# Column sums by way of device memory instead of a TensorE fold, and a twelve-pass lead before each product in halves

## Chip, cores and metric

The program runs on one NeuronCore of a Trainium2 chip. The metric is device time in microseconds (us) of one execution. Three runs of the kernel before took 979.87, 979.88 and 977.43 us, median 979.87. Line numbers such as L113 are lines of the kernel's file; the names of tiles are those of the program.

## What is computed

A two-layer trunk on 256 tokens of width 1024, in fp32. Each layer has a half-step SwiGLU FFN (width 2816), a token mixer (a causal spatial gating part beside sparse attention over selected tokens), and a second FFN. Each of the three is normalised before, shifted and scaled before, and gated behind, by vectors that come from a conditioning vector c:

```python
c_act = jax.nn.silu(c)
for l in range(DEPTH):                                  # DEPTH = 2
    mod = c_act @ ada_w[l] + ada_b[l]                   # (1, 9 * 1024)
    sh1, sc1, g1, sh2, sc2, g2, sh3, sc3, g3 = jnp.split(mod, 9, axis=-1)
    h = modulate(rms_norm(x, norm_ffn1[l]), sh1, sc1)   # h * (1 + scale) + shift
    x = x + 0.5 * g1 * swiglu(h, ffn1_w_in[l], ffn1_w_out[l])
    h = modulate(rms_norm(x, norm_mix[l]), sh2, sc2)
    x = x + g2 * token_mix(h, cos, sin, mix_w_in[l], sgu_w[l], sgu_b[l], mix_w_out[l])
    h = modulate(rms_norm(x, norm_ffn2[l]), sh3, sc3)
    x = x + 0.5 * g3 * swiglu(h, ffn2_w_in[l], ffn2_w_out[l])
return rms_norm(x, final_norm)
```

## The kernel before

**Tiles and phases.** The 256 tokens are two row blocks b = 0, 1 of 128, which stay on the chip in x. Six phases follow each other: FFN 1, mixer and FFN 2 of layer 0, then of layer 1. A matrix product in fp32 is made as three passes of rounded operands (mm3, L594): with hi a rounded copy and lo the remainder, hi x hi, hi x wlo and lo x whi are added up in one PSUM bank. So each weight tile arrives by DMA (raw), is cast by ScalarE to whi (L535) and has its remainder wlo made by VectorE (L540). At most ten such pairs (NB) are in use, seven raw tiles (NRAW) in flight.

**FFN.** It has two stages. In the first, chunks of 512 or 256 columns of w_in are multiplied for gate and up parts. Most are "joint chunks": the weight tile stands still in the PE array, the transposed tokens of both row blocks (256 columns) move, and one matmul takes about 0.11 us. In all phases but the first, one chunk is done apart for each row block, with the weights moving in 512 columns (L741). Its results, transposed, are aThi and aTlo. The second stage ("a-stage") is the down-projection w_out: 22 k-blocks x 2 row blocks x 2 halves of 512 columns x 3 passes, the activations standing and the weights moving. It is written in project (L682), which takes one k-block after another, the second row block some blocks behind the first (LAG), and does the last three (TAIL) half by half so that the update of x can start on one half while the other is multiplied. In the very last down-projection the second row block has its 1024 columns cut in 512, 256 and 256 (PARTS, L601).

**Order of columns in a pass.** For projections the kernel uses mm3r (L577). Its moving operand and its PSUM target are read in an order of their own, by runs (L572): four runs, each of 16 groups of 8 columns, shown as 4x16x8. Twice a row is otherwise: a "product in halves" (L580 to L584) has its first pass in plain order, its second cut in two matmuls of 256 columns, its third by runs. The counter T.n tells whether any other matmul has come between. Behind such a break the first product is done by runs and the next in halves, and on an unbroken stream a product in halves comes every 48 passes (PERIOD). The mixer's projections, other than its output, use plain mm3.

**Modulation vectors.** Sixteen of the 18 vectors (each 1024 long) are made while the phases run; the first two at the start. Their weights are units in the same sequence as the layer weights (weave, L300): eight tiles of 128x1024 a vector, multiplied by c on VectorE into one accumulator aacc (L522; the first of the eight on ScalarE, L517). What is left then is a sum over the 128 partitions of aacc. The kernel before makes it in three steps: VectorE reduces groups of 32 with a transpose (fold_rows, L409; L414), giving a 128x32 tile; TensorE multiplies that with fold, a matrix that adds up the four groups (L430 for a gate, L462 for a shift or scale); VectorE takes the result out of PSUM. Shift and scale vectors go into ab, laid along partitions (L466 to L470). A gate vector gets its bias added, is written to device memory as one row and read back to all partitions by the POOL queue (L433 to L437), giving vec, which update (L644) multiplies with.

**What sets the order.** Each engine runs its instructions in the order in which the program issues them (the schedule is manual). The program is a loop of items: an item is one step of a row block or one step of a joint chunk. Work that must come later is deferred by a number of items (defer, L355), and FOLD_D = (2, 2, 10) are such numbers: the reduce two items behind the last accumulate, the fold ten items behind the reduce. Tiles hThipad and hTlopad are three small slots of 32 columns each, taken in turn. SyncE's queue carries the weights; ScalarE's and POOL's queues carry little.

## Time and profile before

| | us |
|---|---|
| median of three runs | 979.87 |
| the profiled execution, its own time | 978.13 |
| the profiled execution, span from first to last instruction | 976.4 |
| start and first FFN's chunks, 0 to 147.91: length, PE busy | 147.91, 139.73 |
| mixer of layer 0, 209.60 to 322.29: length, PE busy | 112.69, 112.58 |
| FFN 2 chunks of layer 0, 322.29 to 437.41: length, PE busy | 115.12, 115.12 |
| FFN 1 chunks of layer 1, 498.37 to 620.73: length, PE busy | 122.36, 122.36 |
| mixer of layer 1, 681.00 to 793.00: length, PE busy | 112.00, 111.89 |
| FFN 2 chunks of layer 1, 793.00 to 908.37: length, PE busy | 115.37, 115.37 |
| behind the last down-projection, 969.00 to 976.40: length, PE busy | 7.40, 0.38 |

The four down-projections lie between these rows. Over the span the DMA engines moved 253.47 MB, 260 GB/s on average. PE is TensorE's matmuls, PEld its weight loads, DVE is VectorE, ACT ScalarE, POOL GpSimd, SP SyncE. A row of the trace in order of time has the start in us, the duration in us, the engine, the line, the operation, the tiles (out<-in) and the shapes. The durations of neighbouring matmuls overlap, so what a matmul costs is read from one start to the next.

### The profile page before, as it was taken

The page shows a single profiled execution, that of the slowest core. Times are in us where ns is not written, and L with a number is a line of the kernel's source. Part 1 is how long each engine was busy: PE and PEld are TensorE (multiplying, and loading weights), DVE is VectorE, ACT ScalarE, POOL GpSimd, SP SyncE. Part 2 cuts the span into 40 slices and gives each one's busy share as a digit, 9 for nine tenths or more (in the row PEclk, how much of TensorE's full clock was granted, in tenths as well). Part 3 has the DMA queues.
Part 4 walks back from the last instruction along what each step waited for, and adds up shares of the span by engine and source line. Part 5 has one row for each costly group of instructions (what it writes and reads, how often), then busy time and mean ns, then how long its engine had stood idle before and what let it go on. Part 6 is the DMA issues. An engine that isn't in the chain of part 4 may idle for free.

```text
span 976.4 us, 16690 instructions
## 1 busy us (share of the span) xinstructions
PE 961.0 (98%) x6448; PEld 866.6 (89%) x6448; DVE 768.7 (79%) x1072; ACT 530.1 (54%) x794; POOL 54.8 (6%) x92
## 2 busy tenths in 40 slices
PE   7999999999999999999999999999999999999997
PEld 6899998887888899998889999988777889999886
DVE  6889899788998888786587898767899886656444
ACT  6565555375676754553366554345657775444331
POOL 4012400000000100000000100000000000000000
PEclk9999999999999999999999999999999999999999
DMA  9989999967665799897868999885765557777431
GB/s 330 393 277 364 337 385 377 413 178 230 185 181 172 229 329 348 314 328 252 262 185 299 329 332 318 302 301 173 246 189 184 170 175 250 247 239 235 151 129 43
DMA packets 110416, 253.47 MB, mean 260 GB/s; under 512 B 9138, under 2 KB 27620, under 8 KB 110336
## 3 DMA queue, kind: packets, MB, share of 16 engines
q1 hardware_dynamic: 108256, 248.06, 74.6%
q0 software_dynamic: 1792, 3.82, 1.2%
q8 instruction: 50, 0.82, 0.3%
q10 hardware_dynamic: 288, 0.52, 0.1%
q14 instruction: 30, 0.25, 0.1%
HBM read 251.30 MB, written 1.07 MB: 258 GB/s over the span
## 4 chain that ended last, share of the span: by engine, by line
PE 85%; DVE 6%; DMA 4%; issue 2%; ACT 1%; POOL 0%; SPq 0%; POOLq 0%; DVEq 0%; ACTq 0%
PE bank L113 83%; PE bank L117 2%; DMA raw<-in_ffn_w_in_dram 2%; DVE wlo L540 2%; DMA sraw<-in_ada_w_dram 1%; DVE aacc L1195 1%; DVE aacc L522 1%; ACT whi L535 1%; DMA raw<-in_ada_w_dram 1%; DVE xm L645 0%; DVE xm L635 0%; DVE x L647 0%; DVE wlo L481 0%; POOL rstd L618 0%; DVE hTlo L641 0%
## 5 line engine op out<-in xcount | busy, mean ns | idle before, releaser
L535 ACT ACTIVATE whi<-raw 128x1024 fp32r<-128x1024 f32 (+1 forms) x328 | 340.2, 1050 | 261.9 <-PE bank L113 167.1
L540 DVE TENSOR_TENSOR wlo<-raw,whi 128x1024 fp32r<-128x1024 f32 (+1 forms) x313 | 375.1, 1211 | 112.1 <-ACT whi L535 110.6
L113 PE MATMUL bank<-hThi,whi 128*128 128x256 f32 x1216 | 325.0, 278 | 1.4 <-ACT hThi L1233 0.9
L113 PE MATMUL bank<-hThi,wlo 128*128 128x256 f32 x1216 | 322.0, 276 | 0.0
L113 PE MATMUL bank<-hTlo,whi 128*128 128x256 f32 x1216 | 322.0, 276 | 0.0
L113 PEld LDWEIGHTS bank<-hThi,whi 128*128 128x128 f32 x1216 | 222.4, 188 | 3.5 <-ACT hThi L1233 1.5
L113 PEld LDWEIGHTS bank<-hTlo,whi 128*128 128x128 f32 x1216 | 222.1, 188 | 0.1
L113 PEld LDWEIGHTS bank<-hThi,wlo 128*128 128x128 f32 x1216 | 222.0, 188 | 0.0
L522 DVE SCALAR_TENSOR_TENSOR aacc<-raw,ccol,aacc 128x1024 f32<-128x1024 f32 x112 | 143.5, 1281 | 0.0
L113 PE MATMUL bank<-whi,aThi 128*128 128x512 f32 (+1 forms) x374 | 141.0, 377 | 0.0
L113 PE MATMUL bank<-whi,hThi 128*128 128x512 f32 (+1 forms) x352 | 140.4, 399 | 0.0
L113 PE MATMUL bank<-wlo,aThi 128*128 128x512 f32 (+1 forms) x404 | 140.1, 359 | 0.0
L113 PE MATMUL bank<-whi,aTlo 128*128 128x512 f32 (+1 forms) x374 | 139.8, 374 | 0.0
L113 PE MATMUL bank<-whi,hTlo 128*128 128x512 f32 (+1 forms) x352 | 135.4, 385 | 0.2
L113 PE MATMUL bank<-wlo,hThi 128*128 128x512 f32 (+2 forms) x374 | 134.3, 369 | 0.0
L113 PEld LDWEIGHTS bank<-wlo,aThi 128*128 128x128 f32 x404 | 75.9, 188 | 13.0
L113 PEld LDWEIGHTS bank<-wlo,hThi 128*128 128x128 f32 x374 | 70.5, 188 | 12.1
L113 PEld LDWEIGHTS bank<-whi,aTlo 128*128 128x128 f32 x374 | 70.3, 188 | 11.1
L113 PEld LDWEIGHTS bank<-whi,aThi 128*128 128x128 f32 x374 | 70.2, 188 | 10.9
L113 PEld LDWEIGHTS bank<-whi,hTlo 128*128 128x128 f32 x352 | 66.1, 188 | 14.0 <-DVE hTlo L641 1.1
L113 PEld LDWEIGHTS bank<-whi,hThi 128*128 128x128 f32 x352 | 66.3, 188 | 13.6 <-issue 2.0
L798 DVE TENSOR_TENSOR xm<-xm,bank 128x256 f32<-128x256 f32 x76 | 29.6, 417 | 38.8 <-ACT xm L797 38.8
(166 smaller groups left out, 680.9 us busy)
## 6 DMA issues: line engine op xcount, KB each, us to landing
raw<-in_ffn_w_in_dram SPq DMA_DIRECT2D x160, 512.0 KB, 5.4
raw<-in_ada_w_dram SPq DMA_DIRECT2D x128, 512.0 KB, 5.5
raw<-in_ffn_w_out_dram SPq DMA_DIRECT2D x88, 512.0 KB, 5.8
raw<-in_mix_w_in_dram SPq DMA_DIRECT2D x40, 512.0 KB, 4.4
sraw<-in_ada_w_dram SPq DMA_DIRECT2D x32, 256.0 KB, 5.8
raw<-in_ffn_w_in_dram SPq DMA_DIRECT2D x32, 256.0 KB, 4.2
raw<-in_mix_w_out_dram SPq DMA_DIRECT2D x16, 512.0 KB, 4.1
vec<-gline POOLq DMA_DIRECT2D x6, 512.0 KB, 7.2
```

Of the source, the lines that this page charges most:

```text
L113: return nc.tensor.matmul(*a, **kw)
L117: return nc.tensor.transpose(*a, **kw)
L522: V.scalar_tensor_tensor(aacc, e["raw"], ccol[:, j:j + 1], aacc, op0=ALU.mult, op1=ALU.add)
L535: S.activation(hi[:, :n], src, AF.Copy)
L540: V.tensor_tensor(lo[:, :n], src, hi[:, :n].bitcast(F32), op=ALU.subtract)
L798: V.tensor_tensor(a, a, acc[j][:, 256:], op=ALU.mult)
L1195: V.scalar_tensor_tensor(acc, su[g][j], ccol[:, j:j + 1], su["dps"] if j == PEJ else acc, op0=ALU.mult, op1=ALU.add)
```

## The change

**Column sums.** The matrix fold and its setup are gone. column_sums takes the place of fold_rows: VectorE's transposing reduce (now with columns in another order), then the 128x32 tile R is written to device memory (part), read back with another layout (L419) so that the four groups lie side by side in one partition, and VectorE adds them up (L425). Each of these steps is deferred: FOLD_D = (2, 2, 5, 6) stands for the items up to the reduce, the write, the read-back and the sum. Vectors for shift and scale use POOL's queue for the two transfers, gates ScalarE's. A gate then adds its bias (from cols, no longer loaded apart), is scattered to a row in device memory with elements of 4 bytes (gline, L438), and is read to all partitions two items later (vec, L443), on SyncE's queue in layer 1 and for the third gate of layer 0, on POOL's otherwise. The first two gates of layer 0 wait four items more before the sum (GL). In layer 1 the vectors of FFN 2 are woven to end 12 units earlier (FL).

**Order of columns.** In mm3r, a break now puts SETTLE = 4 products of plain order (twelve passes) ahead, then one product in halves, then runs up to the next break; PERIOD is gone. The mixer's output projection uses mm3, so plain order all through. In the last down-projection the second row block uses two halves of 512 like the others; its second half is cut at the last three k-blocks: what has been added up is put into x early (update), and the three last k-blocks go into fresh banks of 512, 256 and 256 columns.

```diff
-PERIOD = 48
+SETTLE = 4
-FOLD_D = (2, 2, 10)
+FOLD_D = (2, 2, 5, 6)
+GL = 4
+FL = 12
...
-        seq += weave(u3, vl[2], F0, F1)
+        seq += weave(u3, vl[2], F0, F1 - FL * l)
...
-    def fold_rows(acc, then):
-        R = spare_tile(0)
-        blocks = acc.rearrange("p (j r) -> p j r", r=32)
+    def column_sums(acc, eng, then, late=0):
+        R, C = spare_tile(0), spare_tile(1)
 
         def red():
-            V.tensor_reduce(R, blocks, axis=AX.X, op=ALU.add, apply_transpose=True)
-            then(R)
+            V.tensor_reduce(R.rearrange("p (m k) -> p m k", m=4),
+                            acc.rearrange("p (k r m) -> p m k r", m=4, r=32),
+                            axis=AX.X, op=ALU.add, apply_transpose=True)
+            defer(FOLD_D[1], there)
+
+        def there():
+            part = dramp.tile([P, 32], F32, name="part", tag="part")
+            eng.dma_start(part, R)
+            defer(FOLD_D[2], lambda: back(part))
+
+        def back(part):
+            eng.dma_start(C.rearrange("p (g k) -> p g k", g=4),
+                          part.rearrange("(g r) (m k) -> (r m) g k", g=4, m=4))
+            defer(FOLD_D[3] + late, total)
+
+        def total():
+            cs = small.tile([P, KD], F32, name="cs", tag="cs")
+            V.tensor_reduce(cs, C.rearrange("p (g k) -> p k g", g=4), axis=AX.X, op=ALU.add)
+            then(cs, C)
         defer(FOLD_D[0], red)
...
+        def put(cs, C):
+            V.tensor_tensor(C[:, :KD], cs, cols[:, l, v * KD:(v + 1) * KD], op=ALU.add)
+            defer(FOLD_D[1], lambda: out(C))
+
+        def out(C):
+            line = dramp.tile([1, D], F32, name="gline", tag="gline")
+            S.dma_start(line.rearrange("o (k p) -> p (o k)", p=P), C[:, :KD])
+            defer(FOLD_D[2], lambda: spread(line))
+
+        def spread(line):
+            t = vecp.tile([P, D], F32, name="vec", tag="vec")
+            (nc.sync if l or v == 8 else G).dma_start(t, line.to_broadcast([P, D]))
+            vec[(l, "G", v // 3 + 1)] = t
+        column_sums(acc, S, put, GL if l == 0 and v < 8 else 0)
...
-        fresh = T.n != stream[0]
-        if ps.shape[-1] == 512 and not first and (fresh or stream[1] >= PERIOD):
+        if T.n != stream[0]:
+            stream[1] = -SETTLE
+        if stream[1] < 0:
+            mm3(ps, ahi, alo, whi, wlo, first, last)
+        elif stream[1] == 0 and ps.shape[-1] == 512 and not first:
...
             T.matmul(runs(ps), alo, runs(whi), start=False, stop=last)
-            stream[1] = 0
         else:
             mm3(runs(ps), ahi, alo, runs(whi), runs(wlo), first, last)
-            if fresh:
-                stream[0], stream[1] = -1, PERIOD
-                return
-        stream[0] = T.n
-        stream[1] += 3
+        stream[:] = T.n, stream[1] + 1
...
-        parts = PARTS if final and b == 1 else HALF
+        parts, cut = HALF, final and b == 1
...
+            own = cut and h > 0
+            (mm3r if n == KF else mm3)(
+                acc[h], ahi, alo, w[0][:, 0, parts[h]], w[1][:, 0, parts[h]],
+                k == 0 or own and k == n - TAIL, k == n - 1 or own and k == n - TAIL - 1)
...
+        if cut:
+            update(b, l, i, acc[1], HALF[1])
+            give(bk.pop())
+            parts = PARTS
+            bk += [take(), take()]
+            acc = [t[:, :sl.stop - sl.start] for t, sl in zip(bk, parts)]
```

**What moves, in TensorE's order.** First the start of the first FFN's down-projection in layer 0, behind the last joint chunk (the rows `bank<-hThi,wlo`). Before, with L113 the line of the matmul:

```order
L113 MATMUL bank_86<-hThi,wlo 128x256
L113 MATMUL bank_83<-whi,aThi 128x4x16x8
L113 MATMUL bank_83<-wlo,aThi 128x4x16x8
L113 MATMUL bank_83<-whi,aTlo 128x4x16x8
L113 MATMUL bank_80<-whi,aThi 128x4x16x8
L113 MATMUL bank_80<-wlo,aThi 128x4x16x8
L113 MATMUL bank_80<-whi,aTlo 128x4x16x8
L113 MATMUL bank_83<-whi,aThi 128x512
L113 MATMUL bank_83<-wlo,aThi 128x256 x2
L113 MATMUL bank_83<-whi,aTlo 128x4x16x8
L113 MATMUL bank_80<-whi,aThi 128x4x16x8
```

Now, from the third product on (the two ahead of it have the same form in the same two banks; lines are now those of the changed file, where the matmul is L115):

```order
L115 MATMUL bank_86<-whi,aThi 128x512
L115 MATMUL bank_86<-wlo,aThi 128x512
L115 MATMUL bank_86<-whi,aTlo 128x512
L115 MATMUL bank_82<-whi,aThi 128x512
L115 MATMUL bank_82<-wlo,aThi 128x512
L115 MATMUL bank_82<-whi,aTlo 128x512
L115 MATMUL bank_86<-whi,aThi 128x512
L115 MATMUL bank_86<-wlo,aThi 128x256 x2
L115 MATMUL bank_86<-whi,aTlo 128x4x16x8
L115 MATMUL bank_82<-whi,aThi 128x4x16x8
```

Before, the second product behind the joint chunk is the one in halves; now four plain products (two in each bank) stand ahead of it. Second, the same down-projection some ten products later in TensorE's order, where the first gate's fold stood. Before:

```order
L113 MATMUL bank_80<-whi,aThi 128x4x16x8
L113 MATMUL bank_80<-wlo,aThi 128x4x16x8
L113 MATMUL bank_80<-whi,aTlo 128x4x16x8
L113 MATMUL bank_82<-fold,hThipad 32x32
L113 MATMUL bank_83<-whi,aThi 128x512
L113 MATMUL bank_83<-wlo,aThi 128x256 x2
L113 MATMUL bank_83<-whi,aTlo 128x4x16x8
L113 MATMUL bank_80<-whi,aThi 128x4x16x8
L113 MATMUL bank_80<-wlo,aThi 128x4x16x8
L113 MATMUL bank_80<-whi,aTlo 128x4x16x8
```

Now, at about the same place, from the product in halves that follows the transposition of cols (L1254, which breaks the stream in both kernels):

```order
L115 MATMUL bank_86<-whi,aThi 128x512
L115 MATMUL bank_86<-wlo,aThi 128x256 x2
L115 MATMUL bank_86<-whi,aTlo 128x4x16x8
L115 MATMUL bank_82<-whi,aThi 128x4x16x8
L115 MATMUL bank_82<-wlo,aThi 128x4x16x8
L115 MATMUL bank_82<-whi,aTlo 128x4x16x8
L115 MATMUL bank_80<-whi,aThi 128x4x16x8
L115 MATMUL bank_80<-wlo,aThi 128x4x16x8
L115 MATMUL bank_80<-whi,aTlo 128x4x16x8
```

The row with fold is gone, and with it the product in halves behind it; the stream goes on by runs. Third, the gate's way. Before, POOL's order for the first two gates of layer 0 (in_ada_b_dram is the bias, hTlopad the small tile that becomes the row):

```order
L420 DMA hTlopad<-in_ada_b_dram 32x32 x2
L435 DMA gline<-hTlopad 32x32
L437 DMA vec<-gline 128x1024
L435 DMA gline<-hTlopad 32x32
L437 DMA vec<-gline 128x1024
L618 TENSOR_TENSOR rstd<-ms,mhalf 128x1 x4
```

Now the row starts on ScalarE's queue, between the weight casts and the FFN's activations (part and gline lie in device memory):

```order
L557 ACTIVATE aThi<-xm_107 128x512
L523 ACTIVATE whi<-raw 128x1024
L1252 ACTIVATE cols<-bank_83 128x96
L415 DMA part<-hThipad 128x32
L523 ACTIVATE whi<-raw 128x1024
L505 ACTIVATE aacc<-raw,ccol 128x1024
L523 ACTIVATE whi<-raw 128x1024
L419 DMA hTlopad<-part 128x4x8
L523 ACTIVATE whi<-raw 128x1024
L438 DMA gline<-hTlopad 128x8x1
L523 ACTIVATE whi<-raw 128x1024 x5
L438 DMA gline<-hTlopad 128x8x1
```

What were four transfers of POOL's queue for the two gates behind the bias loads are now three transfers of ScalarE's for each gate, ahead of casts that the weights wait for; the two broadcasts (vec) stay on POOL's queue.

More of the change, by code (lines that the diff above doesn't have):

```diff
@@ L151, in trunk @@
     V.memset(negm, 1.0)
-    fold = const.tile([P, P], F32, name="fold")
     mconst = const.tile([P, 16], F32, name="mhalf")
-    mhalf, quarter = mconst[:, :1], mconst[:, 4:8]
+    mhalf = mconst[:, :1]
     G.memset(mhalf, -0.5)
-    def fold_setup():
-        V.tensor_reduce(quarter, ident.rearrange("p (a c) -> p a c", a=4), axis=AX.X, op=ALU.add)
-        V.tensor_reduce(fold[:, :32], ident.rearrange("p (a c) -> p c a", a=4), axis=AX.X, op=ALU.add)
-        V.tensor_copy(fold[:, 32:].rearrange("p (a c) -> p a c", a=3),
-                      fold[:, None, :32].to_broadcast([P, 3, 32]))
     def causal_mask():
@@ L416, in fold_rows @@
         defer(FOLD_D[0], red)
-    def bias_row(e):
-        row = spare_tile(1)[:32]
-        G.dma_start(row, ada_b[e["l"], e["v"] * D:(e["v"] + 1) * D].rearrange("(j r) -> j r", r=32))
-        accs.append(row)
     def ada_finish(e, acc):
         l, v = e["l"], e["v"]
-        row = accs.pop()
-        def go(R):
-            def prod():
-                ps = tp_tile()
-                T.matmul(ps[:32, :32], R, fold[:, :32], start=True, stop=True)
-                def put():
-                    V.tensor_tensor(row, ps[:32, :32], row, op=ALU.add)
-                    line = dramp.tile([1, D], F32, name="gline", tag="gline")
-                    G.dma_start(line.rearrange("o (j r) -> (o j) r", r=32), row)
-                    t = vecp.tile([P, D], F32, name="vec", tag="vec")
-                    G.dma_start(t, line.to_broadcast([P, D]))
-                    vec[(l, "G", v // 3 + 1)] = t
-                evac_later(EV_D, put)
-            defer(FOLD_D[2], prod)
-        fold_rows(acc, go)
+        def put(cs, C):
+            V.tensor_tensor(C[:, :KD], cs, cols[:, l, v * KD:(v + 1) * KD], op=ALU.add)
+            defer(FOLD_D[1], lambda: out(C))
@@ L458, in col_finish @@
     def col_finish(e, acc, late):
-        def go(R):
-            def prod():
-                ps = tp_tile()
-                T.matmul(ps[:, :32], fold, R, start=True, stop=True)
-                def put():
-                    Rk = R.rearrange("p (k m) -> p k m", m=4)
-                    V.tensor_tensor(Rk, ps[:, :32].rearrange("p (k m) -> p k m", m=4),
-                                    quarter[:, None, :].to_broadcast([P, KD, 4]), op=ALU.mult)
-                    cs = small.tile([P, KD], F32, name="cs", tag="cs")
-                    V.tensor_reduce(cs, Rk, axis=AX.X, op=ALU.add)
-                    col_bias(e["l"], e["v"] // 3 + 1, e["kind"], cs, 0)
-                evac_later(EV_D, put)
-            defer(FOLD_D[2] + late, prod)
-        fold_rows(acc, go)
+        column_sums(acc, G, lambda cs, C: col_bias(e["l"], e["v"] // 3 + 1, e["kind"], cs, 0), late)
     late = []
@@ L1339, in start @@
         causal_mask()
-        fold_setup()
     gens = {}
```

3 lines of the change are left out of this document (removed).

## The prediction, before the result was known

> **What bounds the kernel now.** I read the page first: the share of each engine, then the chain that ended last.
>
> ```profile
> span 976.4 us, 16690 instructions
> PE 961.0 (98%) x6448; PEld 866.6 (89%) x6448; DVE 768.7 (79%) x1072; ACT 530.1 (54%) x794; POOL 54.8 (6%) x92
> PE 85%; DVE 6%; DMA 4%; issue 2%; ACT 1%; POOL 0%; SPq 0%; POOLq 0%; DVEq 0%; ACTq 0%
> ```
>
> TensorE is covered for 961.0 of 976.4 us and carries 85% of the chain. It rarely waits, so the time is the sum of the distances from one matmul's start to the next, and an edit counts through the matmuls that it removes and the pace of those that stay. The second view is the busy time by stage, cut at the four FFN down-projections ("a-stages": 264 passes each of 512 columns, 22 k-blocks x 2 row blocks x 2 halves x 3 passes). Behind the stretch stand its length, the busy time (and count) of PE, PEld, DVE, ACT and POOL, the granted clock, the DMA share and GB/s.
>
> ```profile
> 147.91:209.60 61.69, 61.69 (x288) 51.08 (x287) 53.30 (x60) 32.25 (x42) 2.70 (x5) 1.00 0.92 348
> 437.41:498.37 60.96, 60.96 (x286) 50.85 (x284) 41.43 (x48) 27.22 (x36) 2.70 (x5) 1.00 0.78 254
> 620.73:681.00 60.27, 60.27 (x285) 50.97 (x284) 41.76 (x50) 26.80 (x36) 1.62 (x3) 1.00 0.76 247
> 908.37:969.00 60.63, 60.63 (x340) 52.71 (x339) 28.81 (x33) 18.83 (x25) 1.94 (x3) 1.00 0.32 105
> ```
>
> PE never rests there and the granted clock is 1.00, yet the pace is not one number. The third view, TensorE in order of time, shows why. A row "128x256 f32 x2" is a product in halves. From one such row to the next, unbroken, lie 48 passes' worth of work.
>
> ```profile
> 153.34 0.24 PE L117 MATMUL bank<-ident,vec 96*128 96x96 f32 x1
> 153.68 0.40 PE L113 MATMUL bank<-wlo,aThi 128*128 128x256 f32 x2
> 154.93 0.25 PE L113 MATMUL bank<-fold,hThipad 128*32 128x32 f32 x2
> 155.44 0.40 PE L113 MATMUL bank<-wlo,aThi 128*128 128x256 f32 x2
> 166.04 0.40 PE L113 MATMUL bank<-wlo,aThi 128*128 128x256 f32 x2
> 168.61 0.25 PE L113 MATMUL bank<-fold,hThipad 128*32 128x32 f32 x2
> 169.12 0.40 PE L113 MATMUL bank<-wlo,aThi 128*128 128x256 f32 x2
> 180.34 0.40 PE L113 MATMUL bank<-wlo,aThi 128*128 128x256 f32 x2
> 191.39 0.40 PE L113 MATMUL bank<-wlo,aThi 128*128 128x256 f32 x2
> ...
> 204.57 1.04 PE L117 MATMUL bank<-ident,xm 128*128 128x128 f32 x8
> 205.68 0.41 PE L113 MATMUL bank<-wlo,aThi 128*128 128x256 f32 x2
> ```
>
> 155.44 to 166.04 is 10.60 us, 220.8 ns a pass (its halved product included). 169.12 to 180.34 is 11.22 us, 233.8 ns. 180.34 to 191.39 is 11.05 us, 230.2 ns. The same instructions on the same shapes run at three paces, and the pace changes only at a product in halves. So that product chooses a pace, and the stream keeps it until the next one.
>
> What does the choice hang on? Compare a stream that had been running evenly with one just broken. The joint chunks run evenly up to the a-stages at 437.41, 620.73 and 908.37. The product in halves behind each, and one behind a fold:
>
> ```profile
> 439.04 0.40 PE L113 MATMUL bank<-wlo,aThi 128*128 128x256 f32 x2
> 448.20 0.25 PE L113 MATMUL bank<-fold,hThipad 128*32 128x32 f32 x2
> ...
> 479.61 0.40 PE L113 MATMUL bank<-wlo,aThi 128*128 128x256 f32 x2
> 490.82 0.40 PE L113 MATMUL bank<-wlo,aThi 128*128 128x256 f32 x2
> ...
> 622.36 0.40 PE L113 MATMUL bank<-wlo,aThi 128*128 128x256 f32 x2
> 631.52 0.25 PE L113 MATMUL bank<-fold,hThipad 128*32 128x32 f32 x2
> ...
> 910.00 0.40 PE L113 MATMUL bank<-wlo,aThi 128*128 128x256 f32 x2
> 918.40 0.28 PE L113 MATMUL bank<-whi,aThi 128*128 128x256 f32 x1
> ```
>
> Behind the joint chunks 41 passes take 9.16 us, twice the same to 10 ns, and 38 take 8.40 us: 221 to 223 ns, the fast pace all three times (the slow one would need 9.59 us for 41). One pass behind a break anything comes: fast at 155.44, slow at 169.12 and at 479.61 (11.21 us to 490.82).
>
> **The change part by part.** First the lead: behind every break twelve contiguous passes run before the product in halves. Whether contiguous passes settle is seen in the mixer, which runs them already:
>
> ```profile
> 260.26 0.48 PE L113 MATMUL bank<-whi,hThi 128*128 128x512 f32 x1
> ...
> 261.49 0.39 PE L113 MATMUL bank<-whi,hTlo 128*128 128x512 f32 x1
> ...
> 264.21 0.39 PE L113 MATMUL bank<-whi,hTlo 128*128 128x512 f32 x1
> ```
>
> 261.49 to 264.21 is 12 passes in 2.72 us, 226.7 ns without change. So twelve of them bring the stream to one known state, and every product in halves behind them should choose the same pace. No row shows that pace: ends 220.8 and 233.8 ns. I take 220.8, since the settled streams nearest to it, the three above, all went there. 264 passes at 220.8 are 58.29 us a stage. The lead costs 12 x (226.7 - 220.8) = 0.07 us a site, two sites in the middle stages, three in the first, one in the last. Where the eight transposes break a stream, 204.57 to 205.68 is 1.11 us for them and one pass, 0.89 more than a pass, in three stages. The column transpose of the first (153.34 to 153.68) costs 0.12. Stage by stage: 59.51, 59.32, 59.32 and 58.36, the last with 0.1 for its 18 half-width passes at the end: 58.46. Sum 236.6. Before, the four stretches sum to 243.55, and the last ran on some 0.2 us: 243.8. **-7.2 us.** That holds the seven folds inside the stages and the last stage's 256-column passes, which become 512 wide.
>
> Second, the folds go from TensorE. Seven lie in the a-stages and are counted. Six break joint chunks, three the mixer.
>
> ```profile
> 393.44 0.30 PE L113 MATMUL bank<-hThipad,fold 128*128 128x32 f32 x2
> 393.58 0.36 PE L113 MATMUL bank<-hThi,whi 128*128 128x256 f32 x1
> 393.78 0.28 PE L113 MATMUL bank<-hTlo,whi 128*128 128x256 f32 x1
> 393.89 0.28 PE L113 MATMUL bank<-hThi,wlo 128*128 128x256 f32 x1
> ```
>
> 393.44 to 393.78 is 0.34 us for two fold passes and one of the chunk's own, which takes 0.11 in an even stretch (393.78 to 393.89): 0.23 us each. Nine of them: **-2.1 us.**
>
> Third, the mixer's output projection becomes contiguous throughout, and the first FFN chunk gets short leads. One of their longest streams now:
>
> ```profile
> 311.59 0.40 PE L113 MATMUL bank<-wlo,hThi 128*128 128x256 f32 x2
> 322.29 1.03 PE L117 MATMUL bank<-ident,xm 128*128 128x128 f32 x8
> ```
>
> 10.70 us for 47 passes is 227.7 ns: where contiguous passes stand as well. I take 0. If all of some 480 such passes moved to an end of the three paces, it would be -3 or +3 us.
>
> Fourth, VectorE, and the queues.
>
> ```profile
> L414 DVE TRANSPOSE_TENSOR_REDUCE hThipad<-aacc 128x32 f32<-128x1024 f32 x16 | 19.8, 1238 | 0.0
> L469 DVE TENSOR_REDUCE cs<-hThipad 128x8 f32<-128x32 f32 x10 | 1.9, 186 | 0.3
> L466 DVE TENSOR_TENSOR hThipad<-bank,mhalf 128x32 f32<-128x32 f32 x10 | 1.9, 185 | 0.0
> gline<-hTlopad POOLq DMA_DIRECT2D x6, 4.0 KB, 3.6
> 150.00:160.00 10.00, 10.00 (x49) 8.23 (x48) 10.00 (x13) 6.84 (x12) 0.00 (x0) 1.00 1.03 413
> ```
>
> A shift or scale vector loses the 185 ns product and keeps a reduce of the 186 ns kind; a gate vector gains one. That is hidden under TensorE's 98%. The transposing reduce reads another order: 1.24 us as now, at most twice that by my estimate, 16 times. Each vector adds a write and a strided read-back, a gate a scattered write in place of the 3.6 us one. The reads are collected 6 items later (a pass group of 1.3 us in an a-stage, 2.7 us in a chunk), so 8 to 16 us stand against landings of a few us, and the first layer's gates get 4 items more. Behind a waiting ACT issue queue the weight casts, behind POOL's the rstd powers, behind VectorE's sum the weight remainders. I take 0; the far end is in the third rival.
>
> Sum: 978.13 (the profiled execution's own time) - 7.2 - 2.1 = **968.8, called 969**. The runs shown have a median of 979.87, 1.7 above that execution, so a median behind the change may lie as much higher.
>
> One rule speaks against the first term. The Trainium skill (TensorE: Matmul & The Clock Gate, section Back-to-back issue gap) gives a warm pass as columns / 2.4 + 2.5 ns, so 216 ns for 512 whatever stood before it. The rows above differ, 220.8 and 233.8 ns, so here the measurement decides. By that rule no pace could be chosen, and the time would be that of rival 4.
>
> **The rivals.** (1) The settled lead meets the wrong pace, the same one eight times over, since the site is the same. For: no row shows a contiguous lead before halves, and 169.12 shows that the slow pace stays until the next product in halves, of which the change leaves only one per break. 935 passes behind the leads x 13.0 ns = 12.2 us on the forecast: **981.0**, slower than before; at the middle pace 977.6. It decides from 968.8 to 978.13, so at 9.3 us / 935 = 10 ns a pass, above 230.8 ns. Against: three settled starts of three were fast.
>
> (2) One long stream is lost. A 208-pass stream in the first layer follows the column transpose, and a single wait of TensorE can shift it with no later product to mend it. 208 x 9 to 13 ns is 2 to 3 us, with a second stream of 232 some 5: **973**.
>
> (3) The first layer starves. At 150 to 160 us VectorE stands at 10.00 of 10 and the DMA share at 1.03, so no room hides more. Five vectors end there. If a gate's round trip costs the weights as much as a 3.6 us landing and a column vector half of that, and twice 1.2 us of slower reduce is added, it is 2 x 3.6 + 3 x 1.8 + 2.4 = 15 us of delay against the chunk's prefetch; I estimate that 6 of it shows: **975**, 984 if all did. The Trainium skill (DMA: Bandwidth & Descriptors, section Specifications) counts transfers under 512 B as read-modify-write; the gate's 4-byte elements are such, and no row here prices them.
>
> (4) The change doesn't do what it says: pace is not chosen by the halves at all. Then only breaks go: 2.1 us, and seven folds in the stages of which each takes, at 168.61 to 169.12, 0.51 us for itself and one pass, 0.29 more than a pass: 2.0 us. **974**.
>
> **How the numbers follow.** Forecast 0.60, by the three settled starts; own range 966 to 972, with the +/-3 of the third part. Rival 1 0.14, rival 2 0.13, rival 3 0.08, rival 4 0.05. The range is 965.5 to 979.5: it holds the forecast, rivals 2 and 4, most of 3 and the middle pace of 1, and leaves out the slow pace and the tails, some 0.18 in all. 0.3% of 979.87 is 2.9 us, about what a measurement tells from no change: below 976.9 lie the forecast, 4 and nearly all of 2 and half of 3, 0.80; within, most of rival 1 and the upper part of 2 and 3, 0.14; above, rival 1's slow pace with the 1.7 us between the profiled execution and the median, and the tail of 3, 0.06.
>
> **What would show it.** Right: the rows in halves lie only behind twelve contiguous passes, and the passes behind each take 220 ns to the stage's end; the a-stages last 59.5, 59.3, 59.3 and 58.5 us; joint chunks run unbroken. Wrong: an a-stage stretch above 61 us with distances of 230 or 233 ns (rival 1, or 2 if one stage alone), TensorE waiting for a weight remainder or rstd before 210 us (rival 3), paces that change without a break (rival 4).

## The result, and the profile after

| | before | after |
|---|---|---|
| median of four runs each, us | 979.64 | 986.84 |
| range, us | 977.43 to 979.88 | 985.49 to 989.27 |
| ratio after / before, 95% interval | | 1.0079 (1.0066 to 1.0092) |
| profiled execution, its own time, us | 978.13 | 989.27 |

The changed kernel is 0.8% slower; the forecast was 969 us, 1.1% faster. The page of the changed kernel, the lines that answer to the first three shown of before:

```profile
span 987.5 us, 16469 instructions
PE 965.5 (98%) x6320; PEld 865.0 (88%) x6320; DVE 780.0 (79%) x1067; ACT 529.0 (54%) x794; POOL 65.0 (7%) x96
PE 63%; DVE 17%; DMA 11%; issue 4%; ACT 2%; POOL 2%; SPq 0%; ACTq 0%; POOLq 0%; DVEq 0%
```

TensorE's share of the chain that ended last fell from 85% to 63%; VectorE's rose from 6% to 17%, the DMAs' from 4% to 11%. So TensorE waits for data in the a-stages, which it did not before. Busy time by stage, cut at the four a-stages (columns as before: length, PE, PEld, DVE, ACT and POOL busy with counts, granted clock, DMA share, GB/s), shows where:

```profile
151.12:221.24 70.12, 64.60 (x279) 52.23 (x278) 51.64 (x60) 29.79 (x40) 2.98 (x5) 0.95 0.96 286
449.58:510.84 61.26, 60.84 (x276) 50.25 (x275) 42.37 (x50) 26.84 (x36) 0.55 (x1) 1.00 0.86 231
632.86:694.42 61.56, 60.73 (x276) 50.32 (x275) 42.06 (x50) 27.16 (x36) 1.86 (x3) 1.00 0.83 246
922.25:980.38 58.13, 58.13 (x275) 49.72 (x274) 28.09 (x34) 18.82 (x25) 0.86 (x1) 1.00 0.37 100
```

Against the four stretches of before (61.69, 60.96, 60.27, 60.63) that is +8.43, +0.30, +1.29 and -2.50 us. The first a-stage begins 3.21 us later than before; the stretches between the a-stages changed by +0.53, -0.34 and +0.46 us, what follows the last pass by -0.28. The sum is 11.1 us, the difference of the two spans. In three a-stages PE is no longer covered all through, and in the first the granted clock fell to 0.95.

What TensorE waited for is seen in the list of waits from 150 to 215 us (engine and line that waited, for what: us in total, times, longest):

```profile
ACT whi L523 <- DMA raw<-in_ffn_w_out_dram: 20.5, 8, 8.6
DVE wlo L528 <- ACT whi L523: 14.9, 8, 5.5
...
ACT whi L523 <- DVE hThipad L408: 6.7, 1, 6.7
...
PEld bank L115 <- ACT whi L523: 3.2, 2, 2.5
PEld bank L115 <- DVE wlo L528: 3.1, 3, 1.1
```

From the last line up: TensorE for the remainders and the casts, the remainders for the casts, the casts for the weights' DMA. The chain of the same stretch (start, duration, what) shows those DMAs, and the DMA issues their landings:

```profile
173.62 11.43 DMA raw<-in_ffn_w_out_dram
...
187.82 18.01 DMA gline<-hTlopad
```

```profile
raw<-in_ffn_w_out_dram SPq DMA_DIRECT2D x88, 512.0 KB, 5.8
...
part<-hThipad ACTq DMA_DIRECT2D x6, 16.0 KB, 5.0
hTlopad<-part ACTq DMA_DIRECT2D x6, 16.0 KB, 3.9
gline<-hTlopad ACTq DMA_DIRECT2D x6, 4.0 KB, 12.5
```

A gate's row of 4 KB, written as 1024 elements of 4 bytes, lands after 12.5 us in the median and 18.0 at most; as 32 pieces of 128 bytes it had landed after 3.6 (6.8 at most). While the first row is under way the weight tiles take 11.4 to 14.3 us; in the same a-stage of the kernel before none took over 7.9. The same 14 us in both kernels, by stage again; after, with the row issued at 172.06:

```profile
172.06:186.00 13.94, 13.94 (x64) 11.55 (x62) 8.31 (x7) 4.19 (x5) 0.55 (x1) 1.00 1.12 177
```

and before:

```profile
172.00:186.00 14.00, 14.00 (x63) 11.44 (x62) 11.03 (x10) 5.30 (x5) 0.61 (x2) 1.00 1.03 420
```

The DMA engines are no less busy (1.12 against 1.03), but move 177 GB/s in place of 420. TensorE lives from what was fetched ahead, runs dry at 185.6 us and again at 195.3. Behind the second stall it runs at half its pace for a while: TensorE in order of time,

```profile
186.27 0.50 PE L115 MATMUL bank<-whi,aThi 128*128 128x512 f32 x1 [0.25 <-ACT whi L523]
187.53 0.49 PE L115 MATMUL bank<-wlo,aThi 128*128 128x512 f32 x1 [0.76 <-DVE wlo L528]
...
188.08 0.38 PE L115 MATMUL bank<-whi,aThi 128*128 128x512 f32 x1
...
195.34 0.39 PE L115 MATMUL bank<-whi,aThi 128*128 128x512 f32 x1
...
199.19 0.76 PE L115 MATMUL bank<-whi,aThi 128*128 128x512 f32 x1 [2.08 <-ACT whi L523]
...
201.47 0.63 PE L115 MATMUL bank<-whi,aThi 128*128 128x512 f32 x1
201.90 0.63 PE L115 MATMUL bank<-wlo,aThi 128*128 128x512 f32 x1
202.33 0.63 PE L115 MATMUL bank<-whi,aTlo 128*128 128x512 f32 x1
```

Behind the first stall the pace is still 220 ns: 33 passes in 7.26 us from 188.08 on. Behind the second it is 427 ns from pass to pass, eleven passes of it, 2.3 us lost on top of the wait of 2.08. The granted clock was 0.50 there (third number from the end, columns as above):

```profile
199.30:206.00 6.70, 6.20 (x14) 4.53 (x15) 4.15 (x4) 2.12 (x2) 0.00 (x0) 0.50 0.63 105
```

The Trainium skill (TensorE: Matmul & The Clock Gate, section Wait — 56ns, not 53.3ns?) gives 426.7 ns for a pass of 512 columns on the halved clock; the trace agrees.

And the paces? The second a-stage, in order of time: the product in halves behind its lead, the first pass of its first stall, the stream behind its last stall, and the transposes that end it:

```profile
452.54 0.40 PE L115 MATMUL bank<-wlo,aThi 128*128 128x256 f32 x2
...
484.28 0.47 PE L115 MATMUL bank<-wlo,aThi 128*128 128x512 f32 x1
...
494.55 0.38 PE L115 MATMUL bank<-whi,aTlo 128*128 128x512 f32 x1
...
505.84 0.27 PE L119 MATMUL bank<-ident,xm 128*128 128x128 f32 x1
```

144 passes take 31.74 us, 220.4 ns each: the forecast pace. Behind the last stall 49 passes take 11.29 us, 230.4 ns each, to the end of the stream. So the lead does what was forecast, and a stall can undo it, as here; the first stall of the first a-stage did not. In the last a-stage, where nothing stalls, the gain is all there.

### The profile page after: what moved, and what is told of

Its sections match the earlier page's. It is cut to its first block, busy times and chain, and to the rows that moved or that the text cites. A ratio compares the mean times of both kernels' runs of the same rounds, so it can differ in the third digit from the quotient of the medians.

```text
span 987.5 us, 16469 instructions
## 1 busy us (share of the span) xinstructions
PE 965.5 (98%) x6320; PEld 865.0 (88%) x6320; DVE 780.0 (79%) x1067; ACT 529.0 (54%) x794; POOL 65.0 (7%) x96
## 4 chain that ended last, share of the span: by engine, by line
PE 63%; DVE 17%; DMA 11%; issue 4%; ACT 2%; POOL 2%; SPq 0%; ACTq 0%; POOLq 0%; DVEq 0%
PE bank L115 62%; DVE wlo L528 5%; DMA raw<-in_ffn_w_out_dram 4%; DVE aacc L510 3%; DMA gline<-hTlopad 2%; PE bank L119 2%; DMA raw<-in_ffn_w_in_dram 1%; ACT whi L523 1%; DMA sraw<-in_ada_w_dram 1%; DMA part<-hThipad 1%; DVE hThipad L408 1%; DMA raw<-in_ada_w_dram 1%; DVE score L964 1%; DVE aacc L1190 1%; DVE sS L1012 1%
## 5 line engine op out<-in xcount | busy, mean ns | idle before, releaser
L115 PE MATMUL bank<-hThi,whi 128*128 128x256 f32 x1216 | 325.9, 279 | 1.0 <-ACT hThi L1228 0.9
L115 PE MATMUL bank<-hThi,wlo 128*128 128x256 f32 x1216 | 323.6, 277 | 0.0
L115 PE MATMUL bank<-hTlo,whi 128*128 128x256 f32 x1216 | 323.5, 277 | 0.0
L115 PEld LDWEIGHTS bank<-hThi,whi 128*128 128x128 f32 x1216 | 223.0, 188 | 3.0 <-ACT hThi L1228 1.5
L115 PEld LDWEIGHTS bank<-hThi,wlo 128*128 128x128 f32 x1216 | 223.0, 188 | 0.0
L115 PEld LDWEIGHTS bank<-hTlo,whi 128*128 128x128 f32 x1216 | 222.3, 188 | 0.1
L115 PE MATMUL bank<-wlo,aThi 128*128 128x512 f32 (+1 forms) x363 | 138.0, 384 | 3.2 <-DVE wlo L528 3.0
L115 PE MATMUL bank<-whi,aThi 128*128 128x512 f32 (+1 forms) x355 | 137.8, 388 | 2.3 <-ACT whi L523 2.3
L115 PE MATMUL bank<-whi,hThi 128*128 128x512 f32 (+1 forms) x352 | 139.9, 397 | 0.0
L115 PE MATMUL bank<-whi,hTlo 128*128 128x512 f32 (+1 forms) x352 | 135.7, 386 | 1.7 <-DVE hTlo L627 0.9
L115 PE MATMUL bank<-whi,aTlo 128*128 128x512 f32 (+1 forms) x355 | 136.9, 386 | 0.0
L115 PE MATMUL bank<-wlo,hThi 128*128 128x512 f32 (+2 forms) x357 | 135.0, 380 | 0.0
L115 PEld LDWEIGHTS bank<-wlo,aThi 128*128 128x128 f32 x363 | 68.8, 189 | 18.7 <-DVE wlo L528 6.3
L115 PEld LDWEIGHTS bank<-whi,hTlo 128*128 128x128 f32 x352 | 66.1, 188 | 16.8 <-DVE hTlo L558 2.6
L115 PEld LDWEIGHTS bank<-whi,aThi 128*128 128x128 f32 x355 | 67.3, 190 | 15.5 <-ACT whi L523 3.2
L115 PEld LDWEIGHTS bank<-whi,hThi 128*128 128x128 f32 x352 | 66.3, 188 | 15.1 <-issue 2.0
L115 PEld LDWEIGHTS bank<-whi,aTlo 128*128 128x128 f32 x355 | 67.3, 190 | 12.2
L115 PEld LDWEIGHTS bank<-wlo,hThi 128*128 128x128 f32 x357 | 67.2, 188 | 11.5
L792 ACT ACTIVATE xm<-bank 128x256 f32<-128x256 f32 x76 | 26.5, 383 | 65.3 <-PE bank L115 61.0
```

What stands on the lines that cost most here:

```text
L115: return nc.tensor.matmul(*a, **kw)
L792: S.activation(a, acc[j][:, :256], AF.Silu)
```

## The experiments

Two theories of the stalls were tested first. **A**: the write in 4-byte elements holds the DMA engines and starves the weight loads. **B**: ScalarE's casts stand behind ScalarE's own DMA issues, which wait for the reduce and the read-back (the wait of 6.7 us above). All ratios are to the kernel before on the same chip, with 95% intervals.

**The row written as it lies.**

```diff
-            S.dma_start(line.rearrange("o (k p) -> p (o k)", p=P), C[:, :KD])
+            S.dma_start(line.rearrange("o (p k) -> p (o k)", p=P), C[:, :KD])
```

> The changed kernel, but a gate's row is written in the order in which it lies (128 pieces of 32 bytes) instead of as 1024 elements of 4 bytes. The gates' columns are then permuted in the output; the number of transfers, their queues and all waits on them stay. Theory A (the write in 4-byte elements holds the DMA engines and starves the weight loads): that transfer lands in under 5 us instead of 12.5, no weight load of an a-stage takes over 8 us, and the 10.3, 1.2 and 1.5 us that TensorE lost in the first three a-stages go, as do the slower paces behind the stalls: a-stages of about 60, 59.5 and 59.4 us, in all 972 to 977 us. Theory B (ScalarE's casts wait behind its DMA issues, which wait for the reduce and the read-back): the stalls stay, 984 to 988 us.

**Gates on POOL's queue** (column_sums with G in place of S, and the row too).

> The changed kernel with the gates' write, read-back and row on POOL's queue instead of ScalarE's; the row is still 1024 elements of 4 bytes. Theory A (the 4-byte write holds the DMA engines): the weight loads behind it still take some 11 us and TensorE still stalls in the first three a-stages, 983 to 990 us. Theory B (casts wait behind ScalarE's DMA issues): the stalls go, 972 to 977 us.

**The order of columns alone**: the kernel before with mm3r and project of the change.

> The kernel before with the new order of columns alone (four plain products behind a break, no periodic product in halves, plain order in the mixer's output, the new cut in the last down-projection); the folds stay on TensorE, so each fold breaks the stream and gets its own lead. If the lead brings every stream to the 220 ns pace, as the changed kernel's trace shows for four starts of four: a-stages of about 60.3, 60.0, 60.0 and 58.6 us, 974 to 977 us in all. Rival (a lead behind a fold settles elsewhere, at 230 ns and more): a-stages of 61 to 62 us, 979 to 983 us.

**The column sums alone**: the changed kernel with mm3r and project of before.

> The changed kernel with the order of columns of before (a product in halves every 48 passes and as second product behind a break, the old cut at the end); the column sums go through device memory. Theory A or B: the stalls stay, about 10 us in the first a-stage and 1 to 2 us in the next two, against 2.1 us from the folds: 986 to 992 us. Rival (the loss comes with the new order of columns, not with the column sums): 976 to 980 us.

| run | median, us | ratio | a-stages, us |
|---|---|---|---|
| row as it lies | 973.12 | 0.9947 (0.9932 to 0.9962) | 63.51, 59.27, 59.25, 58.17 |
| gates on POOL's queue | 984.58 | 1.0062 (1.0043 to 1.0082) | first three 72.40, 61.56, 59.25 |
| order of columns alone | 974.64 | 0.9965 (0.9954 to 0.9977) | 61.04, 60.40, 60.15, 58.73 |
| column sums alone | 988.48 | 1.0109 (1.0092 to 1.0126) | first three 72.00, 61.16, 60.59 |

Theory A holds in all four: with the row as it lies the loss is gone and 13.7 us with it (the difference of the medians; 1.3%, some 13 us, by the ratios), with another queue it stays in the first two a-stages, and it comes with the column sums and not with the order of columns. The row's landing in the first and the second of these runs:

```profile
gline<-hTlopad ACTq DMA_DIRECT2D x6, 4.0 KB, 3.3
```

```profile
gline<-hTlopad POOLq DMA_DIRECT2D x6, 4.0 KB, 11.0
```

Theory B is not nothing. With the row as it lies, a cast of ScalarE still waits 6.7 us for the gate's reduce, and TensorE stalls from 165.3 to 168.2 us by 2.3 us beyond its pace, so the first a-stage is 63.51 us and not the 60 expected; with the gates on POOL's queue no stall stands there. The order of columns alone came to what was expected of it, 3.7 us, though every fold still breaks a stream. Its first a-stage is 0.7 us over the expected 60.3: behind the first fold no product in halves follows the lead, and that stream stays at 230 ns (58 passes, 156.81 to 170.17 us).

In the first of these runs the gates' columns come out permuted, and so they do below with the 4-byte row in the kernel before and with the longer pieces; the amount of work is the same. Next, the row mended in its right order, the 4-byte write by itself, both mends together, and what it is about 4 bytes.

**The row transposed on VectorE**, four transfers of 32 pieces in all.

```diff
+            X = spare_tile(0)
+            V.transpose(X, C)
...
+            for a in range(4):
+                S.dma_start(line.rearrange("o (k a b) -> (o k) a b", a=4, b=32)[:, a, :],
+                            X[32 * a:32 * a + KD, :])
```

> The changed kernel with a gate's row written in runs of 128 bytes: VectorE transposes the 128x32 tile in blocks of 32x32, and four transfers of 8 partitions each write the row in its right order (32 pieces in place of 1024). All of it stays on ScalarE's queue. Theory A (the 4-byte pieces are the loss): the row lands in under 5 us, the stalls at the rows go as in the run with the row as it lies, 972 to 976 us; the smaller stall at some 165 us, where ScalarE's write of part waits for the 2.05 us reduce while casts stand behind it, stays with about 2.5 us. Rival (the row's place on ScalarE's queue costs, whatever its pieces): four issues in place of one, 980 us and more.

**The 4-byte row alone, in the kernel before.**

```diff
-                    G.dma_start(line.rearrange("o (j r) -> (o j) r", r=32), row)
+                    G.dma_start(line.rearrange("o (r j) -> (o j) r", r=32), row)
```

> The kernel before with one thing added: a gate's row is written as 1024 elements of 4 bytes (so its columns are permuted) in place of 32 pieces of 128 bytes; folds, queue and order of columns as before. Theory A: the row takes 9 to 18 us to land instead of 3.6, the weight loads behind it some 11 us, TensorE stalls in the first a-stage and a little in others: 985 to 993 us. Rival (the scatter costs only where ScalarE's queue carries it, or only with the column sums in device memory): 977 to 980 us.

**Transposed, and on POOL's queue.**

> The changed kernel with both causes mended: the row transposed on VectorE and written in runs of 128 bytes, and the gates' transfers on POOL's queue, so that no weight cast stands behind a transfer that waits for VectorE. If the small stall at 165 us comes from that wait, it goes too and the first a-stage comes to some 59.5 to 60.5 us: 968 to 971 us, what the prediction gave. If it comes from VectorE itself (the reduce of 2.05 us in place of 1.24): the stall stays, 972 to 975 us.

**As many pieces, but longer.**

```diff
+            dump = dramp.tile([KD, P, 16], F32, name="dump", tag="dump")
+            S.dma_start(dump.rearrange("k p c -> p k c"), ident.rearrange("p (k c) -> p k c", c=16))
```

> The run with the row as it lies (gates permuted), with a dummy write of 1024 pieces of 64 bytes to device memory added at each gate, behind the row on ScalarE's queue; nothing reads it. If the number of separate pieces written is what holds the DMA engines, the dummy takes 9 to 18 us like the 4-byte row and the stalls come back: 983 to 988 us. If it is the size of 4 bytes, the dummy lands in 3 to 6 us: 972 to 976 us.

| run | median, us | ratio | a-stages, us |
|---|---|---|---|
| transposed, ScalarE's queue | 975.73 | 0.9962 (0.9948 to 0.9976) | first three 66.62, 59.27, 59.26 |
| before, 4-byte row | 984.12 | 1.0059 (1.0042 to 1.0075) | first three 71.14, 60.96, 60.27 |
| transposed, POOL's queue | 972.48 | 0.9935 (0.9920 to 0.9950) | 61.52, 59.27, 59.26, 58.17 |
| 1024 pieces of 64 bytes added | 973.46 | 0.9943 (0.9928 to 0.9958) | first three 63.88, 59.26, 59.25 |

The one layout of the row makes the kernel before 5.1 us slower, on POOL's queue and with the folds in place; in its trace all of it lies in the first a-stage, the second and third are as they were. The number of pieces is not it; from the DMA issues of the last run and of the one with the 4-byte row:

```profile
dump<-ident ACTq DMA_DIRECT2D x6, 64.0 KB, 3.9
```

```profile
gline<-hTlopad POOLq DMA_DIRECT2D x6, 4.0 KB, 8.9
```

1024 pieces of 64 bytes, sixteen times the bytes, land in 3.9 us in the median, and from 172 to 186 us that run moved 334 GB/s. They are not quite free: the two in the first a-stage took 6.3 and 14.1 us, and behind the second, from 183 to 197.2 us, 368 GB/s moved where the run without them had 406. Yet the medians of the two runs differ by 0.3 us. The Trainium skill (DMA: Bandwidth & Descriptors, section Specifications) counts every transfer under 512 bytes as read-modify-write. These runs don't bear that out as one price for all: 64-byte pieces cost little, 128-byte pieces nothing that shows here, 4-byte ones a lot. Where between 4 and 64 bytes the price begins was not tried, nor 4-byte pieces with room between them.

With both mends the kernel is 0.65% faster than before, the lowest ratio of all that ran, though the intervals of most others overlap with its own. Its first a-stage is 2 us over the forecast, and the rows of its passes say why: VectorE and TensorE in order of time,

```profile
162.81 2.07 DVE L408 TRANSPOSE_TENSOR_REDUCE hThipad<-aacc 128x32 f32<-128x1024 f32 x1
...
165.46 0.38 PE L115 MATMUL bank<-whi,aTlo 128*128 128x512 f32 x1
165.68 0.40 PE L115 MATMUL bank<-whi,aThi 128*128 128x512 f32 x1
166.05 0.50 PE L115 MATMUL bank<-wlo,aThi 128*128 128x512 f32 x1
166.39 0.40 PE L115 MATMUL bank<-whi,aTlo 128*128 128x512 f32 x1
```

Two passes are late by 0.27 us together (0.37 and 0.34 us where 0.22 is the pace), for a remainder that stood behind the gate's reduce of 2.07 us on VectorE. From there to the stage's end 230 ns, 160 passes of it: 0.27 us of stall cost 1.7 us more. Hence two more runs: one with a faster reduce, one with leads again and again.

**The row straight from the sums**: the gate's reduce in the order of before, transposed at once, so that the row comes back with eight neighbours to a partition.

```diff
+                V.tensor_reduce(X, acc.rearrange("p (j r) -> p j r", r=32),
+                                axis=AX.X, op=ALU.add, apply_transpose=True)
+                V.transpose(R, X)
```

> The gates' way in another layout, all on POOL's queue: VectorE reduces in the order of before (contiguous in its inner loop), transposes the 128x32 result at once, and the sums come back with eight neighbouring columns to a partition, so the row is written as it lies (128 pieces of 32 bytes, in its right order). Shift and scale vectors as in the changed kernel. If the 0.3 us stall at 165.7 us in the run with the transposed row on POOL's queue comes from the gate's reduce of 2.07 us: the gate's reduce takes 1.25 us, no stall, the first a-stage keeps its 220 ns pace behind the transposition of cols and lasts 59.3 to 60 us, in all 969 to 971 us. If it comes from elsewhere: 61 to 62 us there and 972 to 974 us in all.

**A lead every 28 products.**

```diff
-        if T.n != stream[0]:
+        if T.n != stream[0] or stream[1] >= AGAIN and not (first or last):
             stream[1] = -SETTLE
```

> The run with the transposed row on POOL's queue, with a new lead (four plain products and one in halves) every 28 products on an unbroken stream. If a stall takes a stream off the 220 ns pace and a lead brings it back: in the first a-stage 230 ns from the stall at some 166 us to the next lead, 220 ns behind it, 60 to 60.8 us in place of 61.5; the other a-stages 0.1 to 0.3 us longer for their two added leads; in all 971 to 972.5 us. If the pace of a stream behind a stall doesn't answer to a lead: 230 ns to the end of the stage, 61.5 us, 972.5 to 973.5 us.

The first took 974.27 us (0.9949, 0.9936 to 0.9961), the second 976.79 us (0.9968, 0.9956 to 0.9981). The gate's reduce in the first, on VectorE in order of time, and the first a-stage of that run:

```profile
166.56 1.25 DVE L412 TRANSPOSE_TENSOR_REDUCE hThipad<-aacc 128x32 f32<-128x1024 f32 x1
```

```profile
151.75:211.29 59.54, 59.54 (x278) 50.52 (x277) 54.38 (x65) 31.87 (x42) 6.12 (x10) 1.00 0.96 359
```

The a-stage is as forecast (59.51), yet it begins at 151.75 us, 5 us later than in the run with both mends, and the sum is no better. In the second, twelve leads of twelve led to 220 ns, but no stall came in that trace, so whether a lead mends a pace that a stall has broken wasn't tested; its first a-stage began late as well, at 150.71. So the late beginning asked for an answer. With leads again and again, the joint chunks of the first FFN ran at 117.8 ns a pass from 51 us to the end, where the kernel before had 113.3: two paces here too, and the changed kernel's own trace has the slow one. With the row straight from the sums they were slow to 95 us, and had begun late besides (51.7 us where other runs have 48).

**The gates' bias loaded later** (the row straight from the sums needs it in a new layout; in that run it was loaded among the first weights), and **breaks added**, three matmuls of 32 columns whose result nothing reads.

```diff
+                    if pi == 0 and q in (1, 12, 24):
+                        ps = tp_tile()
+                        T.matmul(ps[:, :32], ident, ident[:, :32], start=True, stop=True)
+                        give(ps)
```

> The run with the row straight from the sums, its gates' bias loaded behind the start instead of in it (768 pieces of 32 bytes that stood among the first weights). If that load cost the 3.6 us by which that run's joint chunks began to run late (51.7 instead of 48.1 us): the first a-stage begins at 146.6 to 147.5 us where the joint chunks run at 113.3 ns a pass, at 150 to 151 us where they run at 117.8; the a-stages stay at 59.5, 59.3, 59.3 us; in all 969 to 971 us at the one pace, 972.5 to 974 at the other. If the load did no harm: 973 to 975 us again.

> The same kernel with three breaks added to the joint chunks of the first FFN: one fp32 matmul of 32 columns each (two passes, as the removed folds had), whose result nothing reads, at some 51, 82 and 115 us. If breaks of that kind decide the pace of the joint chunks, and set 113.3 ns as behind the folds of the kernel before: whatever the pace ahead of the break, 113.3 ns behind one of them to the stage's end, the first a-stage begins by 147.8 us, 969.5 to 971.5 us in all, 0.7 us of it for the breaks. If the pace doesn't answer to them: as without them, plus 0.7 us, with 117.8 ns kept across a break in some run.

They took 973.96 us (0.9943, 0.9931 to 0.9955) and 974.84 us (0.9950, 0.9936 to 0.9963). The first edit missed its aim, since the load was still issued at 15.4 us. The second, whose breaks came at 68.4, 99.0 and 131.9 us, shows a crossing: rows around the first,

```profile
59.90 0.28 PE L115 MATMUL bank<-hThi,whi 128*128 128x256 f32 x1
...
68.38 0.31 PE L115 MATMUL bank<-ident 128*128 128x32 f32 x2
...
71.35 0.28 PE L115 MATMUL bank<-hThi,whi 128*128 128x256 f32 x1
...
90.39 0.28 PE L115 MATMUL bank<-hThi,whi 128*128 128x256 f32 x1
```

72 passes in 8.48 us are 117.8 ns, 168 in 19.04 us behind the break 113.3. The pace ahead of its other two breaks was 113.3 ns already. The last two runs had the bias beside each gate's sums, without and with two breaks:

> The run with the row straight from the sums, each gate's bias loaded beside its own partial sums (128 pieces of 32 bytes, on POOL's queue behind a wait, so not in the start). The run before it had put the load later in the program only: POOL had nothing to wait for and issued it at 15.4 us, in the start as before. If that load is what brought the joint chunks 2.5 to 3.6 us late at some 50 us: they stand there at 48 to 48.9 us again, and the whole takes 969 to 971 us where the joint chunks run at 113.3 ns, 972 to 974 us where they run at 117.8 ns to the end. If the start was late for another reason: 50.5 us and more again, and 973 to 975 us.

> The same with two breaks of 32 columns in the first FFN's joint chunks, at some 54 and 100 us. If the pace of the joint chunks answers to such breaks, as in the one crossing seen (117.8 ns ahead of 68.4 us, 113.3 ns behind it): 113.3 ns behind each to the next break, the first a-stage begins by 147.5 us, in all 969.5 to 971 us. If that crossing was chance: 117.8 ns behind one of them in this run too, and the median no lower than without breaks.

They took 973.93 us (0.9947, 0.9933 to 0.9962) and 973.35 us (0.9940, 0.9926 to 0.9954). Without breaks the pace was 117.8 ns to 93 us, then, behind four transposes, 113.3; with them 113.3 behind both, but also from 54 us on, ahead of the first, so that run shows no second crossing at an added break. Nor did either answer the question of the late start: the joint chunks stood at 50.0 and 49.8 us where 48 to 49 was expected (51.7, 50.5 and 51.3 us in the three runs with the bias in the start), so the bias was at most a part of the reason, and the rest stays open. And the 1.2 us that TensorE won with the breaks on the way to the a-stage (148.87 against 150.09) it lost there: a stall at 167.8 us, 230 ns behind it, an a-stage of 61.83 in place of 59.56 us. The remainder that it waited for stood behind the gate's reduce, which takes 1.25 us in that run; so the shorter reduce alone doesn't take the stall away. In all nine runs with the column sums in device memory and a mended row (the one on ScalarE's queue with the row transposed left out, 213.3 us), the first a-stage ends between 208.3 and 211.3 us, whether the joint chunks were fast or slow, while it begins between 146.6 and 151.8. That suggests that arriving early there means waiting for a weight; no run set it apart.

## Why the prediction was wrong

**The terms.** The first, -7.2 us in the a-stages at 220 ns, was right in mechanism and size. Twelve plain passes and a product in halves brought every long stream to that pace: four of four in the changed kernel, twelve of twelve with leads again and again. Where nothing stalls the a-stages measure 59.54 (the row straight from the sums), 59.27, 59.25 and 58.17 us (the row as it lies), forecast 59.51, 59.32, 59.32 and 58.46, and the order of columns alone gives 0.35%. In the changed kernel the stalls took it back in three of four a-stages: its trace has +7.5 us in the four together, and +3.6 us outside them in place of -2.1.

**The step that failed** is the fourth, "I take 0" for VectorE and the queues. It priced the gate's write by the nearest row, 3.6 us for 32 pieces of 128 bytes; the same 4 KB in 4-byte elements took 12.5 us, and above all it more than halved what the weights got (177 in place of 420 GB/s). The prediction had this as the far end of the third rival, with a chance of 0.08, a price of 3.6 us a gate and 6 to 15 us in all, and placed the loss where VectorE and the DMA engines were full. The place was right for the first a-stage. The price was not: it let a gate cost the weights no more than a landing of 3.6 us, and the two rows of that a-stage landed after 12.7 and 18.0 us. The prediction named the 4-byte elements as what no row prices, and did not let that widen the range. Removing that one thing took 13.7 us off the changed kernel (986.84 to 973.12; 1.3% by the ratios).

**The reduce**: bounded by twice 1.24 us, measured 2.04 on average over 16. It cost little by its length, but twice it was the last thing that a stall waited for: as a wait on ScalarE's queue (2.3 us) and on VectorE (0.3).

**A stall's second price** stood in the second rival: a single wait shifts a stream with no later product to mend it. It was given 2 to 3 us a stream by itself; in the traces it can come on top of a stall, 1.7 us behind 0.27 in the best run. It doesn't come with every one: the stream kept 220 ns behind the first stall of the changed kernel, and behind 2.2 us of stall in the run with the 64-byte pieces (96 passes from 170.62 to 191.74 us); in the run with the row transposed on ScalarE's queue a stall even brought it from 230 back to 220 ns (36 passes from 184.48 to 192.40 us). PERIOD's products in halves, which the change removed, had let the stream choose anew every 48 passes.

**The folds**, -2.1 us outside the a-stages: with the row as it lies all that lies outside them changed by -1.9 us together, but not where the forecast had it: -1.28 ahead of the first a-stage, where only two folds stood, -0.50, -0.36 and +0.55 in the three stretches between the a-stages, -0.26 behind the last. Why so wasn't looked into. In the first FFN the folds had another effect, which the prediction did not see: they broke the joint chunks' stream, and the traces show 113.3 ns behind each of them. In the changed kernel nothing but four transposes breaks it, and it ran from 54.56 to 88.48 us at 117.8 ns (288 passes in 33.92 us):

```profile
54.56 0.28 PE L115 MATMUL bank<-hThi,whi 128*128 128x256 f32 x1
...
88.48 0.28 PE L115 MATMUL bank<-hThi,whi 128*128 128x256 f32 x1
```

and on to the a-stage. Some 950 passes were slow there, some 35 in the kernel before: 915 x 4.4 ns are 4.0 us, against 3.21 us by which the a-stage begins later. That holds for the traced execution, the slowest of the four. The want of the folds doesn't bring the slow pace by itself: the kernel before ran at 113.3 ns from 51.6 us on, ahead of its first fold in that stream at 103.3, and five runs without folds kept 113.3 ns from 53 us to the a-stage (the row as it lies, column sums alone, transposed on either queue, 64-byte pieces). What was lost with the folds is a break that mends a slow stream: with the order of columns alone 117.8 ns turned into 113.3 at the fold at 105.3 us.

**Left open**: why the five runs with the row straight from the sums have their joint chunks 1.7 to 3.6 us late at some 50 us, what decides which pace a stall leaves, and whether a lead behind a stall restores it. The forecast's 969 us was not reached; the best version stands at 972.5. In its trace some 2.5 us lie at the very end: the last output has landed at 968.3 us, but POOL's closing DRAIN lasts until 971.0, and the span ends 3.5 us behind the landing where the kernel before needs 0.9. The DRAIN instructions of POOL in the best version and in the kernel before (ns, shortest/median/longest; the longest is the closing one):

```profile
L1427 POOLq DRAIN  x3: 46/98/6589, 964.4 to 971.5; - x3
```

```profile
L1429 POOLq DRAIN  x3: 46/93/3326, 971.3 to 976.1; - x3
```

It grows with the transfers issued on POOL's queue: 3.3 us for 32, 3.7 for 36, 5.3 for 56, 5.6 for 60, 6.6 for 72. Only the run with the 4-byte row on POOL's queue leaves the row, with 1.9 us for 54. So the mend by way of POOL's queue seems to have a price of its own, which no run set apart.

## What to carry to other kernels

A write to device memory in single 4-byte elements is priced by what it takes from everyone else: 4 KB of it cut the weight stream by more than half for 13 us, so transpose on an engine first and write runs. When a change adds a form of transfer that no row of the profile shows, its range must reach to what it would cost if it blocked the busiest queue for its whole length. An operation that is removed for its cost may have done a service (here a break that mended the pace of a long stream when it was slow), and a faster stretch ahead of a stretch that waits for data may only move the wait. Work that is moved to another queue may show up again at the end of the kernel, where that queue is closed.

## What the runs showed of the hardware

- 1024 writes of 4 bytes land in 8.9 to 13.0 us (medians of four runs, at most 18.0) on either queue; 1024 writes of 64 bytes in 3.9 us (median, at most 14.1), 128 of 32 bytes in 3.3 (median).
- A pass of 512 columns keeps one of several paces, 220 or 230 ns, until something disturbs its stream; a stall of 0.27 us was enough to go from 220 to 230, one of 2.2 us in another run was not. A pass of 256 columns in the joint chunks has two such paces, 113.3 and 117.8 ns; behind a break of two 32-column passes it was the first each time, in two traces coming from the second.
- Behind a stretch in which TensorE was busy for 1.46 of 4.20 us (195.0 to 199.2), the granted clock was 0.50 for some 6.8 us, and eleven passes took 427 ns each; behind them it was 230 to 240.
- POOL's closing DRAIN took 3.3 us with 32 transfers issued on POOL's queue and 6.6 with 72.
